# Even output projection and gate projection of a two-layer trunk moved into the convolution's pipeline of seven-product groups

## The chip, the cores and the metric

One core of a Trainium2 chip runs the whole kernel in one launch. The metric is the device time of that launch in microseconds (us). A profiled execution gives, beside its time, a span (first to last instruction), the busy time of each engine, and the chain of work that ended last. Engines: PE (TensorE, matmul), PEld (its weight loads), DVE (VectorE), ACT (ScalarE), POOL (GpSimd), SP (SyncE, which here only issues DMAs). Each engine works through its own instructions strictly in the order in which they stand.

## The reference

Two layers over 2048 tokens of width 1024; all float32. The part that the change touches, cut:

```python
# even layer, end
mix = jnp.concatenate([r * silu(g_ret), y_conv * silu(g_conv)], axis=-1)   # (S, 2048)
y = mix @ w_out                                                              # w_out (2048, 1024)
h = h + rms_norm(y, post_norm[0])
# odd layer, beginning
u = rms_norm(h, pre_norm[1])
cq, ckv, k_rope, gate = split_cols(u @ w_in, (384, 256, 64, 1024))
# ... attention o from cq, ckv, k_rope ...
h = h + rms_norm((o * silu(gate)) @ w_out_odd, post_norm[1])
```

## The kernel before, in words

A float32 product is made of three matmuls: each operand is split into a high part (ACT cast) and a low part (DVE subtraction, `split`), and `mm3` (L86 to L89) adds high·high, high·low and low·high. Stages follow each other: input projection with retention (to about 755 us), convolution (to 1326 us), even output projection (to 1699 us), gate projection (to 1874 us), the other odd projections, attention, the last output projection.

The input projection and the convolution are written as groups of seven products. A group computes a 2x2 block product with seven instead of eight multiplications (Strassen-Winograd): the left operand's four blocks `A11..A22` and sums of them `S1..S4`, the right operand's `B11..B22` and sums `T1..T4`. One product is 12 matmuls of 128x128 by 512 columns (four k tiles, three passes), a group is 84. A step of the pipeline (`step`, one per product, "slot" from here on) first emits the 12 matmuls of its product on PE (`product`), then in `slot`: small PE work (`pe_ev`, such as transposes), the preparation of later products (`prep`: DVE low part for four slots ahead, ACT high part for five, SP load for eight), events of that slot (`at`), copies of partial sums out of PSUM (`keep_x`), and what follows on the small PE work. `conv_engine` then adds the pieces of a finished group on DVE. Sums of the left operands are made ahead by POOL in `job`s: load four blocks, four 128x512 additions (`job_ops`), store to DRAM. `change` loads and splits a new set of seven right operands. As PROD orders the products, P4 and P3 of a group are done inside the next group.

The output projection is written plainly: for each of 16 tiles of 128 tokens, 96 matmuls of 512 columns (`y_mm`, L980; 16 k tiles, three passes, two halves), where the tile's `mix` block is split as it comes and the weights stay split in SBUF. `y_post` makes the two norms of a tile: squares on ACT, `rstd_small` (DVE, then `pow` on POOL), scaling and the residual on DVE, stores `h_d`. `y_tr` transposes the normed tile on PE (8 matmuls, L946), copies it out on ACT and stores it by POOL in `u2t_d`. The gate projection takes four blocks of 512 tokens by 8 column tiles by 24 matmuls; `gate_post` applies Silu on ACT and stores by POOL. Then follows the projection to cq, ckv and k_rope ("d1", L1179 and on: `u_dma`, `u_split`, `wd_dma`, `wd_prep`, `d1_mm`).

Of the kernel before, what the change touches and what calls it, by code (L numbers as in the profile page):

```python
# [64 lines left out]
def body(ctx, tc, x, positions, pre_norm, post_norm, w_heads, w_conv, even_conv_w, even_conv_b, ret_gn,  # L65
# [34 lines left out]
    u2t_d = dram.tile([D, S], F32, name="u2t_d")  # L100
# [20 lines left out]
    identb = const.tile([P, P], BF16, name="identb")  # L121
    amaskb = const.tile([P, P], BF16, name="amaskb")
# [55 lines left out]
    with ExitStack() as es:  # L178
# [6 lines left out]
        j8 = base.tile([P, 2050], F32, name="j8")  # L185
# [7 lines left out]
        NQ_ = RQ + len(CQ)  # L193
# [29 lines left out]
        comb = {i: {} for i in range(6)}  # L223
# [5 lines left out]
        def comb_new(G_, n_):  # L229
# [3 lines left out]
            elif G_ == 4:  # L233
# [4 lines left out]
                comb[G_][n_] = [(*a_, 0, 3), (*views(row3[w_], 1024 * o, 1, 512), 3, 1)]  # L238
            else:
# [12 lines left out]
        def group_of(Q):  # L252
            return Q // 8 if Q < RQ else 4 + (Q - RQ) // 16
# [14 lines left out]

        def item_dma(n_):
# [149 lines left out]
        with ExitStack() as rs_:  # L419
# [453 lines left out]
            def conv_engine(t_):  # L873
# [3 lines left out]
                if j < 5:  # L877
                    if not RQ <= p < NQ_:
                        return
# [31 lines left out]
                elif RQ <= Q < NQ_:  # L911
# [14 lines left out]
        with ExitStack() as cs_:  # L926
            cp = cs_.enter_context(tc.tile_pool(name="cp", bufs=1, reuse_waits="tile"))
            jc = [cp.tile([P, 3072], F32, tag="u8", bufs=1, name="jc0"), cp.tile([P, 2048], F32, name="jc1")]
            for i, (kd, a_, b_) in enumerate([("w", q_, 0) for q_ in range(6, 16)] + [("u", 1, k) for k in range(4)]):
                job_at(LAST_SMALL + 1 + 5 * i, job(kd, a_, b_, jc[i % 2]))  # L930
            change(5, RQ + 16, dict(B11=-14, T1=-6, T2=-4, B21=-2, T3=-1, T4=0, B22=2), dict(B11=-8, T1=-1, T2=1, B21=2, T3=4, T4=5, B22=7))
            for t_ in range(LAST_SMALL + 1, len(SEQ)):
                step(t_)


    mps, mes = ExitStack(), ExitStack()
    psm = mps.enter_context(tc.tile_pool(name="psm", bufs=1, space=PSUM, reuse_waits="tile"))
    mid = mes.enter_context(tc.tile_pool(name="mid", bufs=1, reuse_waits="tile"))

    def y_tr(t, u2):  # L940
        uo = mid.tile([P, KT, P], F32, tag="uo", bufs=1, name=f"uo{t}")
        for j in range(2):
            pt = psm.tile([P, 4, P], F32, tag="tr", bufs=2, name=f"up{t}_{j}")
            for i in range(4):
                k = 4 * j + i
                PE.transpose(pt[:, i, :], u2[:, k * P:(k + 1) * P], ident)  # L946
            A.copy(uo[:, 4 * j:4 * j + 4, :], pt)
        G.dma_start(u2t_d[:, t * P:(t + 1) * P].rearrange("(k p) t -> p k t", p=P), uo)
# [856 lines left out]
```

## Time and profile before

| | |
|---|---|
| time, median of 3 runs (lowest to highest) | 3057.41 us (3056.49 to 3058.24) |
| the profiled execution's own time | 3055.22 us |
| its span | 3053.4 us |
| busy: PE, PEld, DVE, ACT, POOL | 97%, 86%, 59%, 45%, 28% of the span |
| mean granted TensorE clock | 0.992 |

The busy share of PE is a sum over matmuls that overlap each other, so it says that PE is hardly ever without work, not that it is at its peak. To read what a stage costs, look at the distance between the starts of matmuls: a 128x512 matmul is listed with 0.39 us, but the next one starts 0.227 us later. The granted clock is 1.0 at 2.4 GHz and 0.5 at 1.2 GHz.

### The profile page before, as it was taken

How to read it: one execution, taken by the hardware profiler on the slowest of the kernel's cores; microseconds unless marked ns; L12 is line 12 of the kernel's file. 1: busy time of each engine (PE TensorE's matmuls, PEld its weight loads, DVE VectorE, ACT ScalarE, POOL GpSimd, SP SyncE). 2: the span in 40 equal slices, each digit the busy share in tenths (PEclk: the TensorE clock that was granted, in tenths of full speed). 3: DMA queues.
4: the chain of work that ended last, by engine and by line, in shares of the span. 5: the costliest groups of instructions: out<-in, count | busy, mean ns of one | idle time of the engine just before them, and what ended most of it. 6: DMA issues, size and time to landing. Idle time of an engine off the chain costs nothing.

```text
span 3053.4 us, 46275 instructions
## 1 busy us (share of the span) xinstructions
PE 2976.4 (97%) x16425; PEld 2615.8 (86%) x16425; DVE 1788.4 (59%) x3557; ACT 1371.5 (45%) x3312; POOL 849.1 (28%) x1203
## 2 busy tenths in 40 slices
PE   7989999999999999989999999999999999999998
PEld 6878889898888888878888888988899999999887
DVE  7767777767665755553323312577666666666643
ACT  5655555656333533332222322333655555555521
POOL 5554455521442000001111110023333333334210
PEclk9999999999999999999999999999999999999999
DMA  7476777756887633354333624246111212111552
GB/s 294 165 245 209 236 239 246 244 168 220 290 300 226 193 111 111 111 179 143 114 125 108 196 77 135 69 137 227 54 60 53 72 53 67 61 60 56 171 171 85
DMA packets 292246, 463.94 MB, mean 152 GB/s; under 512 B 28432, under 2 KB 183712, under 8 KB 287264
## 3 DMA queue, kind: packets, MB, share of 16 engines
q1 hardware_dynamic: 260208, 376.80, 39.2%
q0 software_dynamic: 22128, 74.99, 6.8%
q10 hardware_dynamic: 9680, 9.20, 0.9%
q8 instruction: 130, 2.13, 0.3%
q14 instruction: 100, 0.82, 0.1%
HBM read 322.49 MB, written 158.07 MB: 157 GB/s over the span
## 4 chain that ended last, share of the span: by engine, by line
PE 89%; DMA 4%; POOL 2%; DVE 2%; ACT 1%; issue 1%; SPq 0%; POOLq 0%; DVEq 0%; ACTq 0%
PE y L980 11%; PE bx L87 6%; PE bx L88 5%; PE bx L89 5%; PE fy L1752 5%; PE T L1557 4%; PE by L87 3%; PE by L88 3%; PE by L89 3%; PE o L1587 2%; PE o L1586 2%; PE o L1585 2%; PE S L1504 2%; PE S L1507 2%; PE S L1508 2%; PE S L1505 2%
## 5 line engine op out<-in xcount | busy, mean ns | idle before, releaser
L1525 POOL TENSOR_SCALAR P<-P,al 128x512 f32<-128x512 f32 (+2 forms) x320 | 220.0, 698 | 352.5 <-DVE al L1530 168.1
L307 DVE TENSOR_TENSOR us<-us 128x512 fp32r<-128x512 f32 x392 | 295.9, 760 | 17.4 <-ACT us L299 14.5
L1515 ACT ACTIVATE P<-S,nm 128x512 f32<-128x512 f32 (+2 forms) x320 | 201.1, 628 | 197.1 <-DVE nm L1512 173.5
L299 ACT CAST us<-us 128x512 fp32r<-128x512 f32 x392 | 235.5, 620 | 103.1 <-DMA us<-s_d 31.8
L1512 DVE TENSOR_REDUCE nm<-S 128x1 f32<-128x512 f32 (+2 forms) x320 | 194.4, 609 | 70.6 <-PE S L1508 42.6
L1561 DVE TENSOR_TENSOR TL<-T,TH 128x512 fp32r<-128x512 f32 x224 | 154.4, 689 | 64.0 <-ACT TH L1560 63.1
L1585 PE MATMUL o<-TH,vH 128*128 128x256 f32 x576 | 185.1, 321 | 0.0
L370 ACT COPY u<-bx 128x512 f32<-128x512 f32 (+1 forms) x124 | 66.1, 533 | 236.7 <-PE bx L89 236.5
L980 PE MATMUL y<-woH,mH 128*128 128x512 f32 x512 | 159.9, 394 | 9.4 <-ACT woH L82 9.4
L1557 PE MATMUL T<-ident,P 128*128 128x128 f32 x1088 | 166.2, 273 | 0.0
L1587 PE MATMUL o<-TH,vL 128*128 128x256 f32 x576 | 162.9, 283 | 0.0
L1586 PE MATMUL o<-TL,vH 128*128 128x256 f32 x576 | 162.1, 281 | 0.0
L980 PE MATMUL y<-woH,mL 128*128 128x512 f32 x512 | 158.2, 391 | 0.0
L980 PE MATMUL y<-woL,mH 128*128 128x512 f32 x512 | 157.6, 389 | 0.0
L83 DVE TENSOR_TENSOR mL<-mr,mH 128x512 fp32r<-128x512 f32 (+1 forms) x72 | 45.3, 630 | 170.2 <-ACT mH L82 170.1
L1560 ACT CAST TH<-T 128x512 fp32r<-128x512 f32 x224 | 131.3, 586 | 24.0 <-PE T L1557 18.9
L1557 PEld LDWEIGHTS T<-ident,P 128*128 128x128 f32 x1088 | 125.1, 140 | 7.8
L910 POOL DMA_DIRECT2D mix_d<-j x32 | 17.8, 556 | 375.6 <-DVE j L909 373.6
L82 ACT CAST mH<-mr 128x512 fp32r<-128x512 f32 (+1 forms) x72 | 40.9, 569 | 176.8 <-issue 93.6
L980 PEld LDWEIGHTS y<-woH,mH 128*128 128x128 f32 x512 | 95.4, 189 | 28.6 <-ACT woH L82 9.8
L1504 PE MATMUL S<-kH,aqn 128*128 128x512 f32 (+2 forms) x320 | 118.4, 370 | 0.1
L1507 PE MATMUL S<-K,aqr 128*128 128x512 f32 (+2 forms) x320 | 115.4, 361 | 0.0
(543 smaller groups left out, 9240.6 us busy)
## 6 DMA issues: line engine op xcount, KB each, us to landing
us<-ws_d SPq DMA_DIRECT2D x128, 256.0 KB, 3.4
us<-s_d SPq DMA_DIRECT2D x96, 256.0 KB, 4.7
us<-wc_d SPq DMA_DIRECT2D x96, 256.0 KB, 2.8
us<-a_d SPq DMA_DIRECT2D x72, 256.0 KB, 4.6
qn_d<-qn POOLq DMA_DIRECT2D x32, 512.0 KB, 3.5
aqn<-qn_d SPq DMA_DIRECT2D x64, 256.0 KB, 3.2
mr<-mix_d SPq DMA_DIRECT2D x56, 256.0 KB, 2.7
jc<-in_even_w_conv SPq DMA_DIRECT2D x40, 256.0 KB, 5.0
```

The lines of the kernel that those rows point to most:

```text
L87: PE.matmul(o, ah, bh, start=first, stop=False, **kw)
L88: PE.matmul(o, ah, bl, start=False, stop=False, **kw)
L89: PE.matmul(o, al, bh, start=False, stop=last, **kw)
L299: A.copy(ring[n_][:, 0], f32(ring[n_][:, 1]))
L307: V.tensor_tensor(out=t_[:, 1], in0=src, in1=f32(t_[:, 0]), op=ALU.subtract)
L980: PE.matmul(ys[t][i], a, w[k][:, i * 512:(i + 1) * 512], start=first and pi == 0, stop=last and pi == 2)
L1515: later(D_EXP, lambda: A.activation(p_[:, 0:w], sp[:, 0:w], AF.Exp, bias=nm[:, j:j + 1], accum_out=sm[:, j:j + 1]))
L1525: G.tensor_scalar(t_[:, 0:ww], t_[:, 0:ww], al[:, jj:jj + 1] if n > 1 else al[:, 5:6], al[:, 5:6] if n > 1 else 1.0, op0=ALU.mult, op1=ALU ...
L1557: PE.transpose(tp[:, e, z, :], src, ident)
L1585: PE.matmul(hold[i], vH[h][:, kb, :], pth[:, c], start=first, stop=False)
L1586: PE.matmul(hold[i], vH[h][:, kb, :], ptl[:, c], start=False, stop=False)
L1587: PE.matmul(hold[i], vL[h][:, kb, :], pth[:, c], start=False, stop=last)
```

## The change

- Output projection: 16 groups of seven products (numbers `CE` to `YE` in the slot count), in two passes of 8. The first pass takes k = 0..1023 (the retention half of `mix`) and stores its result in DRAM (`yp_d`). The second takes k = 1024..2047 and adds the first pass's result, loaded back (`p_in`): three of the four 128x512 additions of a group on POOL (`y_out`), one on DVE.
- Gate projection: 8 groups (from `YE`), with the weights as left operand and the transposed tokens as right operand, each half of the tokens one set of right operands.
- The norms of a finished group of the second pass (two token tiles, tA and tB) run as events of the next group's slots: `y_rstd` (ACT square, then on POOL a multiply-add and a `pow`), `y_h` (DVE scale, POOL residual add of 128x1024, POOL store of `h_d`), `y_rstd` again, `y_u2` (DVE), `y_tr` (8 PE transposes, 8 ACT copies, 2 SP stores to `ub2_d`), and once both tiles are stored `y_sum`: four POOL subtractions in place over the transposed tiles, which give the right operand's sums, and four POOL stores to `tu_d`.
- 20 further jobs in the convolution's slots (sums of `w_out`, of the first half of `mix`, of the gate weights), 8 in the first pass (second half of `mix`), and DRAM copies of `w_out` and of the gate weights into blocks.
- Where an own stage began, with its own tiles and loads, the slots now run on.

Cut diff:

```diff
+        CE = RQ + len(CQ)
+        YE = CE + 16
+        NQ_ = YE + 8
...
+            elif Q >= CE:
+                q_, w = divmod(Q - CE, 8)
+                if i in AIX:
+                    r, kh = divmod(AIX[i], 2)
+                    SP.dma_start(L, mix_rows(q_, kh, 2 * w + r))
+                else:
+                    SP.dma_start(flat(L), ms_d[Q - CE, :, SIX0[i]])
...
+            def y_out(p, r, h, t_, eng):
+                if p < CE + 8:
+                    tok = (2 * (p - CE) + r) * P
+                    eng.dma_start(yp_d[tok:tok + P, h * 512:h * 512 + 512], t_)
+                elif p < YE:
+                    yt = yb["p"][r][:, h * 512:h * 512 + 512]
+                    G.tensor_tensor(out=yt, in0=yt, in1=t_, op=ALU.add)
...
+            def y_rstd(t, i, src):
+                ss = base.tile([P, 1], F32, tag="yss", bufs=3, name=f"yss{t}_{i}")
+                A.activation(yb["u"][t % 2], src, AF.Square, accum_out=ss)
+                G.tensor_scalar(ss, ss, 1.0 / D, EPS, op0=ALU.mult, op1=ALU.add)
+                G.tensor_tensor(out=ss, in0=ss, in1=nhalf[:, 0:1], op=ALU.pow)
...
+            def y_h(t):
+                V.scalar_tensor_tensor(out=yb["u"][r], in0=yb["p"][r], scalar=yrs.pop((t, 0)), in1=yb["g"], ...)
+                G.tensor_tensor(out=yb["x"][r], in0=yb["u"][r], in1=yb["x"][r], op=ALU.add)
+                G.dma_start(h_d[t * P:(t + 1) * P, :], yb["x"][r])
+            def y_u2(t):
+                V.tensor_scalar(yb["u"][t % 2], yb["x"][t % 2], yrs.pop((t, 1)), None, op0=ALU.mult)
+            def y_tr(t):
...
+                            PE.transpose(pts[j][:, i, :], yb["u"][h][:, k * P:(k + 1) * P], ident)
...
+                            A.activation(uo[:, k * P:(k + 1) * P], pts[j][:, i, :], AF.Copy, scale=gcol[:, k:k + 1])
+                        SP.dma_start(ub2_d[half, h, j][:, :, w * P:(w + 1) * P], uo[:, j * 512:(j + 1) * 512]...)
+            def y_sum(w2, i):
+                a_, b_ = yb["o"]
+                b11, b21, b12, b22 = a_[:, 0:512], a_[:, 512:1024], b_[:, 0:512], b_[:, 512:1024]
+                o, x_, y_ = ((b11, b12, b11), (b12, b22, b12), (b22, b22, b11), (b21, b21, b22))[i]
+                G.tensor_tensor(out=o, in0=x_, in1=y_, op=ALU.subtract)
+                if i == 3:
+                    for n_, src in (("T1", b11), ("T3", b12), ("T2", b22), ("T4", b21)):
+                        G.dma_start(tu_d[half, :, TIX[n_], :, w * P:(w + 1) * P], src...)
...
+            for w in range(8):
+                b = T0(CE + 8 + w)
+                n = b + 7
+                at(n - 1, lambda tB=tB: x_in(tB))
+                at(n + 2, lambda tA=tA: x_in(tA))
+                at(n + 2, lambda tB=tB: y_rstd(tB, 0, yb["p"][1]))
+                at(n + 3, lambda tB=tB: y_h(tB))
+                at(n + 5, lambda tB=tB: y_rstd(tB, 1, yb["x"][1]))
+                at(n + 6, lambda tB=tB: y_u2(tB))
+                small(n + 7, *y_tr(tB))
+                at(n + 4, lambda tA=tA: y_rstd(tA, 0, yb["p"][0]))
+                at(n + 5, lambda tA=tA: y_h(tA))
+                at(n + 7, lambda tA=tA: y_rstd(tA, 1, yb["x"][0]))
+                at(n + 8, lambda tA=tA: y_u2(tA))
+                small(n + 9, *y_tr(tA))
+                for i in range(4):
+                    at(n + 10 + i // 2, lambda w=w, i=i: y_sum(w, i))
...
+            for G_, Q in ((6, CE), (7, CE + 8), (8, YE), (9, YE + 4)):
+                change(G_, Q, L6, S6)
...
-        for t in range(NB0, NT):
-            y_alloc(t)
-            nxt = []
-            for k4 in range(4):
-                h, l = cur[k4]
-                for i in range(4):
-                    y_mm(t, h[:, i, :], l[:, i, :], 4 * k4 + i, k4 == 0 and i == 0, k4 == 3 and i == 3)
...
-        for tb in range(4):
-            UH, UL = ubt[tb][:, 0], ubt[tb][:, 1]
-            for c in range(8):
...
-                for k in range(KT):
-                    mm3(pp, H[:, k, :], L[:, k, :], UH[:, k, :], UL[:, k, :], k == 0, k == KT - 1)
```

What the change makes of POOL's order. Before, in the output projection, POOL had these rows for two token tiles (`yrs`: the norms' `pow`; `u2t_d`: store of a transposed tile; `h_d`: store of the residual):

```order
L128 TENSOR_TENSOR yrs_12935<-yrs_12935,nhalf 128x1
L998 DMA h_d<-hh_12930 128x1024
L128 TENSOR_TENSOR yrs_12935<-yrs_12935,nhalf 128x1
L948 DMA u2t_d<-uo_13008 128x8x128
L128 TENSOR_TENSOR yrs_13090<-yrs_13090,nhalf 128x1
L998 DMA h_d<-hh_13085 128x1024
L128 TENSOR_TENSOR yrs_13090<-yrs_13090,nhalf 128x1
L948 DMA u2t_d<-uo_13163 128x8x128
```

The elementwise work of the stage was on DVE. Now, in the second pass, a group's round on POOL begins with these rows (L1085 is `y_sum` of the group before, in place on the transposed tiles `uo`; `yx` is the residual and holds tB in the first row of L1052; `yss` are the norms):

```order
L1085 TENSOR_TENSOR uo<-uo 128x512 x2
L1052 TENSOR_TENSOR yx<-yu,yx 128x1024
L1053 DMA h_d<-yx 128x1024
L998 TENSOR_TENSOR yp<-yp,u_75_14212 128x512
L1085 TENSOR_TENSOR uo<-uo 128x512 x2
L1089 DMA tu_d<-uo 128x4x128 x4
L1045 TENSOR_SCALAR yss_0_14411<-yss_0_14411 128x1
L1046 TENSOR_TENSOR yss_0_14411<-yss_0_14411,nhalf 128x1
L1045 TENSOR_SCALAR yss_1_14435<-yss_1_14435 128x1
L1046 TENSOR_TENSOR yss_1_14435<-yss_1_14435,nhalf 128x1
```

and ends with these (the residual of tA, its second norm, two additions of the next group and the first norm of the next tB), after which the next round's L1085 stands:

```order
L1052 TENSOR_TENSOR yx<-yu,yx 128x1024
L1053 DMA h_d<-yx 128x1024
L1045 TENSOR_SCALAR yss_1_14491<-yss_1_14491 128x1
L1046 TENSOR_TENSOR yss_1_14491<-yss_1_14491,nhalf 128x1
L998 TENSOR_TENSOR yp<-yp,u_76_14462 128x512
L998 TENSOR_TENSOR yp<-yp,p_76_14291 128x512
L1045 TENSOR_SCALAR yss_0_14556<-yss_0_14556 128x1
L1046 TENSOR_TENSOR yss_0_14556<-yss_0_14556,nhalf 128x1
L1085 TENSOR_TENSOR uo<-uo 128x512 x2
```

So the subtractions of one group stand ahead of the norms of the next group on the same engine.

## Rows read from the trace of the kernel before

**Rows 1.** The page: busy time, and PE and its clock in 40 slices.
```profile
PE 2976.4 (97%) x16425; PEld 2615.8 (86%) x16425; DVE 1788.4 (59%) x3557; ACT 1371.5 (45%) x3312; POOL 849.1 (28%) x1203
...
PEclk9999999999999999999999999999999999999999
```
**Rows 2.** Busy time by stretch: length, engines, granted clock, DMA share, GB/s.
```profile
760.00:1000.00 240.00, 240.00 (x1061) 198.79 (x1060) 144.75 (x193) 90.00 (x157) 90.19 (x82) 1.00 0.83 269
1000.00:1326.00 326.00, 325.32 (x1435) 268.81 (x1433) 179.01 (x273) 123.53 (x217) 11.48 (x26) 1.00 0.42 125
1340.00:1700.00 360.00, 360.00 (x1650) 299.19 (x1649) 131.27 (x195) 107.39 (x211) 39.67 (x60) 1.00 0.44 144
1875.00:1895.00 20.00, 17.90 (x102) 15.95 (x101) 6.98 (x11) 8.43 (x21) 1.26 (x2) 1.00 0.63 193
```
**Rows 3.** PE's timeline at two borders of stages: start, length, instruction, idle before.
```profile
1325.94 0.39 PE L89 MATMUL by<-row,us 128*128 128x512 f32 x1
1335.71 2.08 PE L980 MATMUL y<-woH,mH 128*128 128x512 f32 x4 [9.38 <-ACT woH L82]
...
1874.05 0.32 PE L87 MATMUL pa<-wdH,ut 128*128 128x352 f32 x1
```
**Rows 4.** The chain of waits, one token tile: start, length, what.
```profile
1415.41 0.88 PE up L946 x8
1416.28 21.81 PE y L980 x96
```
**Rows 5.** Stretches of 2 us around the wait at 1326 us, as rows 2.
```profile
1326.00:1328.00 2.00, 0.33 (x2) 0.00 (x0) 1.52 (x3) 0.63 (x1) 0.00 (x0) 1.00 0.34 131
1328.00:1330.00 2.00, 0.00 (x0) 0.00 (x0) 0.46 (x1) 0.00 (x0) 0.54 (x1) 0.62 0.07 29
1336.00:1338.00 2.00, 2.00 (x5) 1.55 (x5) 2.00 (x3) 1.10 (x3) 0.00 (x0) 0.50 0.64 246
1338.00:1340.00 2.00, 2.00 (x9) 1.64 (x8) 1.31 (x3) 1.35 (x2) 0.00 (x0) 0.82 0.94 296
```
**Rows 6.** POOL by shape: line, operation, count, busy us, mean ns, idle before.
```profile
L376 POOL TENSOR_TENSOR jc<-jc 128x512 f32<-128x512 f32 x46 | 64.0, 1392 | 19.0 <-DMA jc<-a_d 16.7
L332 POOL TENSOR_TENSOR c2B<-c2B 128x768 fp32r<-128x768 f32 x2 | 4.6, 2290 | 0.0
L948 POOL DMA_DIRECT2D u2t_d<-uo x16 | 14.8, 928 | 76.5 <-ACT uo L947 70.2 <-issue 6.3
L998 POOL DMA_DIRECT2D h_d<-hh x16 | 9.5, 593 | 48.0 <-DVE hh L997 48.0
```
**Rows 7.** POOL's small norm steps: duration ns min/median/max, first and last start.
```profile
L462 POOL TENSOR_SCALAR ss<-ss x16: 189/234/1917, 7.4 to 157.1; 128x1 f32<-128x1 f32 x16
L463 POOL TENSOR_TENSOR ss<-ss,nhalf x16: 550/560/1470, 7.7 to 157.4; 128x1 f32<-128x1 f32 x16
```
**Rows 8.** DVE and ACT by shape, columns as rows 6.
```profile
L1001 DVE SCALAR_TENSOR_TENSOR u<-hh,yrs,gpre 128x1024 f32<-128x1024 f32 x16 | 20.6, 1285 | 11.0 <-POOL yrs L128 11.0
L171 DVE TENSOR_SCALAR nsinT<-sinT 128x512 f32<-128x512 f32 x1 | 0.4, 426 | 0.0
L332 DVE TENSOR_TENSOR c4T<-c4T 128x1024 fp32r<-128x1024 f32 x8 | 9.8, 1222 | 2.8 <-ACT c4T L331 2.6
L914 DVE TENSOR_TENSOR p<-ba,p 128x512 f32<-128x512 f32 x30 | 20.6, 687 | 32.2 <-PE ba L89 32.2
L537 ACT COPY kT<-tr 128x128 f32<-128x128 f32 x64 | 17.1, 267 | 0.7
L331 ACT CAST c4T<-c4T 128x1024 fp32r<-128x1024 f32 x8 | 8.4, 1052 | 0.0
```
**Rows 9.** DMA issues, 1340 to 1720 us: count, KB each, median us to landing.
```profile
mr<-mix_d SPq DMA_DIRECT2D x56, 256.0 KB, 2.7
u2t_d<-uo POOLq DMA_DIRECT2D x16, 512.0 KB, 4.1
u2r<-u2t_d SPq DMA_DIRECT2D x8, 512.0 KB, 6.4
```

More of the change, by code (lines that the diff above doesn't have):

```diff
@@ L99, in body @@
     h_d = dram.tile([S, D], F32, name="h_d")
-    u2t_d = dram.tile([D, S], F32, name="u2t_d")
+    yp_d = dram.tile([S, D], F32, name="yp_d")
+    ub2_d = dram.tile([2, 2, 2, P, 4, 512], F32, name="ub2_d")
+    tu_d = dram.tile([2, P, 4, 4, 512], F32, name="tu_d")
+    ty_d = dram.tile([2, P, 4, 4, 512], F32, name="ty_d")
+    wo_d = dram.tile([2, 2, 2, P, 4, 512], F32, name="wo_d")
+    ms_d = dram.tile([16, P, 4, 512], F32, name="ms_d")
+    gs_d = dram.tile([4, P, 4, 512], F32, name="gs_d")
+    wg_d = dram.tile([8, 2, P, 512], F32, name="wg_d")
     gate_d = dram.tile([D, S], F32, name="gate_d")
@@ L222, in body @@
             crow3[n_] = ((9, o_["B11"])[i // 3], i % 3)
-        comb = {i: {} for i in range(6)}
+        comb = {i: {} for i in range(10)}
         row3 = {}
@@ L877, in conv_engine @@
                 if j < 5:
-                    if not RQ <= p < NQ_:
+                    if not RQ <= p < CE:
                         return
@@ new lines, in y_u2, with pe, en @@
+            def y_u2(t):
+                V.tensor_scalar(yb["u"][t % 2], yb["x"][t % 2], yrs.pop((t, 1)), None, op0=ALU.mult)
+            def y_tr(t):
+                half, w, h = t // 8, (t % 8) // 2, t % 2
+                def pe():
+                    pts = [psb.tile([P, 4, P], F32, tag=tag, bufs=1, name=f"up{t}_{tag}") for tag in ("tr", "sk")]
+                    for j in range(2):
+                        for i in range(4):
+                            k = 4 * j + i
+                            PE.transpose(pts[j][:, i, :], yb["u"][h][:, k * P:(k + 1) * P], ident)
+                    return pts
+                def en(pts):
+                    uo = yb["o"][h]
+                    for j in range(2):
+                        for i in range(4):
+                            k = 4 * j + i
+                            A.activation(uo[:, k * P:(k + 1) * P], pts[j][:, i, :], AF.Copy, scale=gcol[:, k:k + 1])
+                        SP.dma_start(ub2_d[half, h, j][:, :, w * P:(w + 1) * P], uo[:, j * 512:(j + 1) * 512].rearrange("p (k t) -> p k t", k=4))
+                return pe, en
@@ L932, in body @@
+            at(T0(CE) + 6, y_open)
+            at(T0(CE + 8) + 3, y_tiles)
+            at(T0(YE) + 7, g_open)
             for t_ in range(LAST_SMALL + 1, len(SEQ)):
                 step(t_)
-    mps, mes = ExitStack(), ExitStack()
+    mps = ExitStack()
     psm = mps.enter_context(tc.tile_pool(name="psm", bufs=1, space=PSUM, reuse_waits="tile"))
[L938 to L943, printed above, removed]
-            for i in range(4):
[L945 to L948, printed above, removed]
@@ L1133, in body @@
-    mes.close()
     with ExitStack() as oes:
@@ L1168, in body @@
             with ExitStack() as es1:
-                ep = es1.enter_context(tc.tile_pool(name="ep", bufs=1, reuse_waits="tile"))
+                ep = es1.enter_context(tc.tile_pool(name="ep", bufs=1, side="right", reuse_waits="tile"))
                 NQ = QL + KVL + ROPE
@@ L1191, in u_dma @@
                     urr[t] = ep.tile([P, KT, P], F32, tag="ur", bufs=2, name=f"ur{t}")
-                    SP.dma_start(urr[t], u2t_d[:, t * P:(t + 1) * P].rearrange("(k p) t -> p k t", p=P))
+                    for j in range(2):
+                        w = (t % 8) // 2
+                        SP.dma_start(urr[t][:, 4 * j:4 * j + 4, :], ub2_d[t // 8, t % 2, j][:, :, w * P:(w + 1) * P])
                 def u_split(t):
```

297 lines of the change are left out of this document (134 added, 163 removed).

## The prediction, written before the changed kernel ran

> **What bounds the kernel now.** I read the page first: PE is busy 97% of the span, and its clock is full in all 40 slices [rows 1]. So nothing but PE's own work, or a new wait of PE, can move the time much. Then the stretches by stage: PE has no idle time in the convolution nor in the output projection, while POOL works 40 of 360 us in the latter [rows 2]. Then PE's timeline at the borders: the last convolution matmul starts at 1325.94 us, the first of the output projection at 1335.71 after 9.4 us of waiting, the first of d1 at 1874.05 [rows 3]. The chain of waits shows a steady token tile: 96 matmuls in 21.81 us and 8 transposes in 0.88 [rows 4]. That is 0.227 us a matmul, and it is the price of every 512-column matmul below.
>
> **PE's own work.** From the end of the convolution (1325.94 + 0.23) to d1 are 547.9 us. The new stretch has 16 + 8 groups of 84 matmuls, 288 fewer than before, and the same 16 times 8 transposes: 24 x 84 x 0.2272 = 458.0, and 16 x 0.88 = 14.1, together 472.1 us. The gain is 75.8 us, of which 65 are matmuls and the rest the 9.4 us wait with the slow matmuls behind it [rows 3, 5]. This holds only if PE never waits. A group with its 16 transposes takes 19.08 + 1.76 = 20.8 us; this is the pace that the other engines must keep in the second pass.
>
> **First pass and gate groups.** They carry no norms. POOL does at most one job (four additions of 1.39 us [rows 6]) in six slots of 2.7 us, and DVE and ACT have less to do than in the convolution, which ran without a PE wait at a DMA share of 0.83 while the jobs ran [rows 2]. The 20 jobs added there prolong that state, they do not thicken it. I cost all this at nothing; it is hidden behind PE, and if the cover fails, a rival below has the price.
>
> **Second pass: a loop through POOL.** POOL's own work in a round is seven 128x512 operations (9.7 us at 1.39), two of 128x1024, four pairs of small norm steps (0.23 + 0.56 each [rows 7]), two stores of 0.59 and four stores to `tu_d`. For 128x1024 there is no row: not below the 2.29 of 768 columns, and 3.2 if 512 to 768 is extended [rows 6]; I take 2.6, a little under twice the 1.39 of the 512-column row, which is much the larger sample. A `tu_d` store lies between the 0.59 of `h_d` and the 0.93 of `u2t_d`, which has twice its pieces; I take 0.72. The sum is 9.7 + 5.2 + 3.2 + 1.2 + 2.9 = 22.2 us, already over 20.8. But the order makes it worse, since POOL also waits in it: `y_sum` of one group stands ahead of the residual and norms of the next group, and it overwrites `uo`, so it waits until the stores of `uo` to `ub2_d` have landed. Those come last in a chain that began with the very norms that POOL still has to do. Following one round from `y_sum`'s start:
> - POOL: four subtractions, one addition (5 x 1.39 = 6.96), residual of tB 2.6, store 0.59, four `tu_d` stores 2.9, first norm of tA 0.79: 13.8 us.
> - DVE, in order behind that norm: scaling of tA 1.29, a sum out of PSUM 0.69, a low part of about the same form (0.69), then `y_u2` of tB. The last has no row at 1024; twice the 512-column 0.426 is 0.85, the ends are 0.43 and the 1.29 of the scaling [rows 8]. Together 3.5 us. The second norm of tB is done by POOL meanwhile.
> - PE: transposes of tB 0.88, two products 5.45 (they stand between tB and tA), the first four transposes of tA 0.44: 6.8 us.
> - ACT: four copies of 0.267 [rows 8] before the first store: 1.1 us.
> - SP's store of 256 KB in 512-byte pieces: 2.7 as the equally large `mix_d` loads, 4.1 as the twice as large `u2t_d` stores, 6.4 as the `u2r` loads of that stretch [rows 9]. I take 3.4, between the first two, which are nearest in kind.
>
> That is 28.6 us against 20.8. PE stands for the difference in front of tB's transposes: after tA's transposes it has five products (13.6 us) and then nothing, for about 7 to 8 us. Behind it wait all later products, whose inputs are ready. In the 9.4 us wait of before the clock fell to half within 2 to 4 us of the last matmul and was back to full about 3 us after the next [rows 5]; 3.2 us at half rate lose 1.6 us. A wait of 7 us should do the same. The round is then 30.2 us and loses 9.4.
>
> How often: the first group's norms have no `y_sum` ahead of them, so its transposes come in time. From tA of the first to tA of the eighth group are seven rounds: 7 x 9.4 = 66 us. In the last two rounds the split of the gate's first right operands stands among the norms on DVE (1.22 each [rows 8]): one such step in the sixth, and in the seventh a product's operand itself comes late, some 3 us; I add 4.
>
> The Trainium skill ("GPSIMD Engine Reference", section 3.1, Elementwise — side-by-side cycle accounting) speaks against this change: it calls VectorE about twice as fast for elementwise two-input work and gives 4.5 us for an addition of 2048 columns on GpSimd, so, as an estimate from that page, 1.12 for 512 and 2.25 for 1024. The row has 1.39 for 512 [rows 6], beside a busy DVE, so the row decides. By the page's figures a round would be 1.7 us shorter and the time 12 us less, 3043.
>
> **Border to d1.** Before, d1's first operands were ready when the gate ended, and PE lost 20 - 17.9 = 2.1 us later on weights [rows 2]. Now ACT's casts for d1 stand behind the last gate Silu, which waits for PE's last product: DVE sum 0.69, Silu and its store about 1 (an estimate, from the 1.05 of a cast twice as wide), cast of `ut` 1.05 and of `wd` 0.72, then two DVE low parts of 1.22 and 0.84, of which half lies beside ACT (0.72 and 0.84 are scaled from 1024 to 704 columns) [rows 8]. PE loses some 5.5 us, so 3.4 more than before; the bounds are 0 (loads early enough to hide all weights' waits) and 7.
>
> **Sum.** -75.8 + 66 + 4 + 3.4 = -2.4 us. On the profiled execution's 3055.2 that is 3052.8; the median of the runs lies 2.2 above that execution, so 3055.
>
> **Rivals.**
> - *The loop does not bind.* For it: POOL is idle for 320 of 360 us in this stage now, DVE for 229 [rows 2], and PE would only have to wait if POOL is behind. Against it: the order, in which the subtractions precede the next residual, and 22.2 us of POOL work in 20.8. It needs a round under 20.8, so 8 us off the chain; no row is off by so much. Time: 3057.4 - 75.8 + 3.4 = 2985. Between this and my forecast lie rounds of 21 to 27 us.
> - *The loop holds, and its store lands late: slower.* The second pass moves about 7 MB a round (7 operand loads of 256 KB, two loads and a store of 512 KB for each of two tiles, eight stores of 256 KB), over 200 GB/s, more than the 144 of this stretch before [rows 2]. If the store to `ub2_d` takes the 6.4 us of the `u2r` loads, each round is 3 us longer: 21 us more, 3076. It decides from 4.6 us of landing on (1.2 us more in seven rounds bring the time over the bound of "slower").
> - *The convolution starves.* The added jobs and DRAM copies could make left operands late in the second half of the convolution, where DMA had fallen to 0.42. If each of the 20 jobs cost one slot of 2.7 us: 54 us more, 3109. Against it: 760 to 1000 us, the same jobs, PE idle for nothing [rows 2].
> - *The clock holds*, since the waits are shorter than the one of before: 1.6 us a round less, 11 in all, 3044. This is inside my own range.
>
> **How the numbers follow.** The loop binds with its landing near the rows: 0.62, own range 3038 to 3068, from a landing of 2.7 with the clock held (round 27.9, 7 x 7.1 = 50 us) to one of 4.6 with the 1024-column operation at 3.2. The loop does not bind, or hardly: 0.12. Late landing: 0.20. Starved convolution or another new wait: 0.06. A run of this kernel can be told from no change from about 0.2% on, 6.1 us. Faster (below 3051.3): the 0.12 and somewhat over a third of the 0.62, 0.35. Within: 0.26, the largest part of what is left of the 0.62. Slower: 0.39. The range that leaves two in ten outside goes from 3030 to 3085.
>
> **What would show it.** In the profile after: PE gap-free from the convolution into the first pass; then in the second pass PE waits seven times, 6 to 9 us each, released by DVE's `y_u2` (tB), with transposes of tB about 30 us apart and the granted clock at half behind each wait; POOL's longest wait is `y_sum` on the store to `ub2_d`. Gate groups of 19.1 us without waits. I am wrong if the second pass runs at about 21 us a group, if PE waits there for left operands or for PSUM, or if the convolution has waits that it had not.

## The result: slower by 1.5%, and the profile after

| | before | after |
|---|---|---|
| median of the runs on the same chip | 3056.95 us (4 runs) | 3105.2 us (4 runs, 3101.15 to 3105.42) |
| ratio after to before | | 1.0154, interval 1.0137 to 1.0172 |
| profiled execution; span; clock | 3055.22; 3053.4; 0.992 | 3105.31; 3103.2; 0.980 |

The forecast was 3055, range 3030 to 3085: the time lies 50 us above it and outside the range. The page of after, answering [rows 1]: 22.8 us less PE work, 301 us more on POOL, and a dip of the granted clock around slice 20.

```profile
PE 2953.6 (95%) x16137; PEld 2580.9 (83%) x16137; DVE 1972.6 (64%) x3697; ACT 1504.5 (48%) x3596; POOL 1150.3 (37%) x1427
...
PEclk9999999999999999999988899999999999999999
```

By stretch, as [rows 2] (length; PE, PEld, DVE, ACT, POOL; clock, DMA share, GB/s): the convolution (1000 to 1326), the first pass, five rounds of the second pass, its end, the gate groups.

```profile
1000.00:1326.00 326.00, 318.25 (x1384) 260.58 (x1383) 207.28 (x268) 124.78 (x216) 106.67 (x90) 0.99 0.80 255
1340.00:1480.00 140.00, 137.50 (x599) 111.75 (x598) 77.56 (x90) 54.29 (x94) 54.62 (x53) 1.00 0.98 303
...
1560.00:1680.00 120.00, 94.31 (x385) 75.50 (x384) 56.36 (x60) 53.10 (x132) 83.39 (x86) 0.87 0.72 219
1680.00:1790.00 110.00, 78.53 (x316) 61.02 (x315) 56.45 (x64) 57.87 (x127) 69.96 (x67) 0.84 0.76 253
1790.00:1890.00 100.00, 97.33 (x420) 78.18 (x419) 50.69 (x71) 54.70 (x92) 5.93 (x6) 1.00 0.76 234
```

PE waits for a fifth to over a quarter of the second pass, and the granted clock is 0.84 to 0.87 there. The convolution, which had no wait, has 7.7 us of them, at nearly twice the DMA share it had (0.80 against 0.42 in [rows 2]). The three largest waits of PE in the second pass (engine, line, waited for: us, times, longest). The first is product P7 waiting for ACT's copy of a partial sum, the second tB's transposes, the third product P2 (bank `ba`) waiting for a right operand's high part:

```profile
PE bx L87 <- ACT u L403: 37.7, 7, 8.6
PE up_tr L1066 <- DVE yu L1056: 10.8, 5, 2.9
PE ba L87 <- ACT c4T L364: 10.6, 1, 10.6
```

and the two largest of POOL in the same stretch:

```profile
POOL uo L1085 <- DMA ub_d<-uo: 54.5, 8, 11.1
POOL yss L1045 <- ACT yu L1044: 18.1, 13, 3.1
```

The 54.5 us are `y_sum` waiting for the stores of `uo` to land: the loop that was forecast. One round of it, from POOL's timeline (start, length, instruction, idle before and its releaser). It begins and ends with `y_sum`:

```profile
1646.46 3.09 POOL L1085 TENSOR_TENSOR uo<-uo 128x512 f32<-128x512 f32 x2 [4.83 <-DMA ub_d<-uo]
1649.51 2.36 POOL L1052 TENSOR_TENSOR yx<-yu,yx 128x1024 f32<-128x1024 f32 x1
...
1660.41 0.56 POOL L1046 TENSOR_TENSOR yss<-yss,nhalf 128x1 f32<-128x1 f32 x1
1661.05 1.28 POOL L1045 TENSOR_SCALAR yss<-yss 128x1 f32<-128x1 f32 x1
1662.42 0.55 POOL L1046 TENSOR_TENSOR yss<-yss,nhalf 128x1 f32<-128x1 f32 x1
1662.93 2.76 POOL L1052 TENSOR_TENSOR yx<-yu,yx 128x1024 f32<-128x1024 f32 x1
...
1679.48 1.66 POOL L1085 TENSOR_TENSOR uo<-uo 128x512 f32<-128x512 f32 x1 [4.88 <-DMA ub_d<-uo]
```

The same round on DVE,

```profile
1661.00 1.29 DVE L1051 SCALAR_TENSOR_TENSOR yu<-yp,yss 128x1024 f32<-128x1024 f32 x1 [13.97 <-POOL yss L1046]
1662.20 0.68 DVE L1036 TENSOR_TENSOR p<-ba,p 128x512 f32<-128x512 f32 x1
1662.81 0.68 DVE L336 TENSOR_TENSOR us<-us 128x512 fp32r<-128x512 f32 x1
1663.40 2.84 DVE L1056 TENSOR_SCALAR yu<-yx,yss 128x1024 f32<-128x1024 f32 x1
```

on ACT (the square at 1654.14 ends ACT's wait for POOL; the copy at 1655.19 behind it is the one that PE waits for),

```profile
1654.14 1.06 ACT L1044 ACTIVATE yu<-yp 128x1024 f32<-128x1024 f32 x1 [8.93 <-POOL yp L998]
1655.10 0.18 ACT L1044 ACTIVATION_READ_ACCUMULATOR yu<-yp 128x1 f32 x1
1655.19 0.57 ACT L403 COPY u<-bx 128x512 f32<-128x512 f32 x1
...
1674.98 1.14 ACT L1074 ACTIVATE uo<-up_tr,gcol 128x128 f32<-128x128 f32 x4 [1.28 <-issue]
```

on PE, at its two waits and at tA's transposes,

```profile
1655.81 0.79 PE L87 MATMUL bx<-c4B,us 128*128 128x512 f32 x1 [5.27 <-ACT u L403]
...
1666.30 0.66 PE L1066 MATMUL up_tr<-ident,yu 128*128 128x128 f32 x4 [2.54 <-DVE yu L1056]
...
1674.29 0.60 PE L1066 MATMUL up_tr<-ident,yu 128*128 128x128 f32 x4
```

and the store on SP:

```profile
1676.14 2.07 SPq L1075 DMA_DIRECT2D ub_d<-uo  x2
```

The clock behind PE's first wait, as stretches of 2 us:

```profile
1656.00:1658.00 2.00, 2.00 (x5) 1.61 (x6) 0.00 (x0) 1.83 (x4) 1.60 (x3) 0.50 0.01 2
...
1662.00:1664.00 2.00, 1.75 (x8) 1.09 (x6) 2.00 (x4) 0.11 (x1) 1.92 (x3) 1.00 0.38 109
```

Read it as a chain in which each engine waits for the one before: POOL 14.5 us (1646.46 to 1660.97), DVE 5.3 (to 1666.24), PE 8.7 (to ACT's copies at 1674.98, with the first product at the half clock), ACT 1.2, store 3.3 (1676.14 to 1679.48): 33.0 us, against 30.2 forecast and 20.8 wanted.

**The ledger**, from starts of matmuls on PE's timeline. The seven rounds, transposes of tA to transposes of tA, take 31.2, 33.5, 32.2, 33.0, 31.0, 38.8 and 36.2: 235.9 us, 90.0 more than 7 x 20.84. Where right operands change, groups stand further apart than 19.1: 11.2 us lost in the convolution (30.5 from group to group; 19.3 before), 4.0 at the first pass, 4.2 at the second, 4.7 inside the gate. The norms of the second pass's first group, ahead of the seven rounds, lose 2.5, most of it PE waiting at P7. d1's first matmul waits 4.3. Together 120.9 us of losses, less the 75.8 of PE work: 45.1 of the 49.1 us by which d1 starts later (1923.16, against the 1874.05 of [rows 3]); the rest is spread.

### The profile page after: what moved, and what is told of

Its sections match the earlier page's. It is cut to its first block, busy times and chain, and to the rows that moved or that the text cites. A ratio compares the mean times of both kernels' runs of the same rounds, so it can differ in the third digit from the quotient of the medians.

```text
span 3103.2 us, 47313 instructions
## 1 busy us (share of the span) xinstructions
PE 2953.6 (95%) x16137; PEld 2580.9 (83%) x16137; DVE 1972.6 (64%) x3697; ACT 1504.5 (48%) x3596; POOL 1150.3 (37%) x1427
## 4 chain that ended last, share of the span: by engine, by line
PE 76%; DMA 7%; POOL 6%; issue 5%; DVE 4%; ACT 2%; SPq 1%; POOLq 0%; ACTq 0%; DVEq 0%
PE bx L87 7%; PE bx L88 7%; PE bx L89 7%; PE fy L1783 5%; PE by L87 4%; PE T L1588 4%; PE by L88 4%; PE by L89 4%; PE o L1617 2%; PE o L1618 2%; PE o L1616 2%; PE S L1535 2%; PE S L1538 2%; PE S L1539 2%; PE S L1536 2%
## 5 line engine op out<-in xcount | busy, mean ns | idle before, releaser
L336 DVE TENSOR_TENSOR us<-us 128x512 fp32r<-128x512 f32 x560 | 460.8, 831 | 70.1 <-ACT us L328 66.8
L328 ACT CAST us<-us 128x512 fp32r<-128x512 f32 x560 | 339.5, 623 | 203.9 <-DMA us<-wc_d 38.1
L1546 ACT ACTIVATE P<-S,nm 128x512 f32<-128x512 f32 (+2 forms) x320 | 200.7, 627 | 196.7 <-DVE nm L1543 173.1
L403 ACT COPY u<-bx 128x512 f32<-128x512 f32 (+1 forms) x172 | 94.0, 546 | 293.8 <-PE bx L89 293.5
L409 POOL TENSOR_TENSOR jc<-jc 128x512 f32<-128x512 f32 x138 | 198.5, 1438 | 42.2 <-DMA jc<-in_even_w_out 14.6
L87 PE MATMUL bx<-c4T,us 128*128 128x512 f32 x384 | 152.8, 398 | 1.7 <-ACT c4T L364 1.0
L88 PE MATMUL bx<-c4T,us 128*128 128x512 f32 x384 | 151.5, 394 | 1.0 <-DVE c4T L365 0.8
L89 PE MATMUL bx<-c4T,us 128*128 128x512 f32 x384 | 151.1, 393 | 0.0
L1535 PE MATMUL S<-kH,aqn 128*128 128x512 f32 (+2 forms) x320 | 118.4, 370 | 0.1
L1538 PE MATMUL S<-K,aqr 128*128 128x512 f32 (+2 forms) x320 | 115.5, 361 | 0.0
L1536 PE MATMUL S<-kL,aqn 128*128 128x512 f32 (+2 forms) x320 | 115.3, 360 | 0.0
L1539 PE MATMUL S<-K,aqr 128*128 128x512 f32 (+2 forms) x320 | 115.2, 360 | 0.0
L1537 PE MATMUL S<-kH,aqn 128*128 128x512 f32 (+2 forms) x320 | 115.0, 359 | 0.0
```

Source lines behind the costliest of these rows:

```text
L87: PE.matmul(o, ah, bh, start=first, stop=False, **kw)
L88: PE.matmul(o, ah, bl, start=False, stop=False, **kw)
L89: PE.matmul(o, al, bh, start=False, stop=last, **kw)
L328: A.copy(ring[n_][:, 0], f32(ring[n_][:, 1]))
L336: V.tensor_tensor(out=t_[:, 1], in0=src, in1=f32(t_[:, 0]), op=ALU.subtract)
L1546: later(D_EXP, lambda: A.activation(p_[:, 0:w], sp[:, 0:w], AF.Exp, bias=nm[:, j:j + 1], accum_out=sm[:, j:j + 1]))
```

## The experiments

Measured times are medians beside runs of the kernel before on the same chip; the seven rounds are read as above, from the one profiled execution of each run. Names of waits: P7 is the product of the first wait in the list above. A theory or rival keeps its letter through all expectations.

| run | time, us | ratio to before, interval | seven rounds, us |
|---|---|---|---|
| changed kernel | 3105.2 | 1.0154, 1.0137 to 1.0172 | 235.9 |
| e1_nosub | 3037.3 | 0.9934, 0.9916 to 0.9951 | 168.0 |
| e2_sep | 3099.7 | 1.0141, 1.0126 to 1.0156 | 213.1 |
| e3_late | 3089.1 | 1.0108, 1.0093 to 1.0123 | 200.7 |
| e4_rstd | 3115.9 | 1.0197, 1.0181 to 1.0212 | 248.4 |
| e5_stt | 3106.8 | 1.0161, 1.0146 to 1.0176 | 239.7 |
| e6_jobs | 3101.4 | 1.0144, 1.0126 to 1.0162 | 236.1 |
| e7_dve | 3066.7 | 1.0034, 1.0022 to 1.0045 | 183.0 |
| e9_best | 3067.5 | 1.0036, 1.0025 to 1.0046 | 185.5 |
| e10_gap40 | 3100.0 | 1.0142, 1.0128 to 1.0155 | 233.3 |
| e11_ring9 | 3039.6 | 0.9947, 0.9932 to 0.9962 | 172.2 |
| e12_best | 3035.2 | 0.9929, 0.9916 to 0.9941 | 172.2 |

### The loop

**e1_nosub.**
```diff
-                G.tensor_tensor(out=o, in0=x_, in1=y_, op=ALU.subtract)
```


> Left out: the four POOL subtractions of y_sum in each of the eight groups of the second pass; the four stores to tu_d stay and carry unsummed blocks, so the gate's sums are wrong. All transfers stay. Theory L (the loop: y_sum waits on POOL for the stores of uo to have landed, and the next group's norms wait behind it): without the write in place the stores to tu_d need only ACT's copies, the chain per round falls from about 33 to under 20, and the rounds of the second pass go back to about 21 to 22 us instead of 31 to 39: 75 to 90 us less, 3015 to 3030. Rival A (ACT's order: the copy of a finished product's partial sum stands behind the square of tA, which waits for POOL's addition): most of the 5 to 6 us wait in front of product P7 stays in each round, about 35 to 45 us of the 90: 3060 to 3070. Rival D (full DMA queues): the traffic is the same, so the rounds stay at 31 to 39 us: 3100 to 3110.

Five rounds of 22.0 to 22.2 us, then 28.1 and 29.5; 67.9 us less in the rounds and as much in the time, which at 3037.3 lies above the 3015 to 3030 of theory L. Five rounds are where L put them, and rivals A and D fall: the wait at P7 is gone and the traffic is all there. But the edit also takes the subtractions' own work from POOL (4 x 1.34 us a round), so it does not tell the wait from that work; e2 and e3 do. The last two rounds were to be 21 to 22 and are not. The DMA share is near 1 in the five rounds already and 1.03 with the gate's right operands on top (stretches as above); in the last two rounds PE waits for the high and low parts of those operands:

```profile
1628.00:1650.00 22.00, 21.10 (x101) 17.31 (x102) 15.06 (x16) 13.96 (x35) 17.83 (x20) 1.00 0.96 321
...
1670.00:1680.00 10.00, 6.74 (x22) 4.99 (x21) 6.46 (x7) 6.39 (x14) 3.52 (x4) 0.66 1.03 401
```

**e2_sep.**
```diff
-                o, x_, y_ = ((b11, b12, b11), (b12, b22, b12), (b22, b22, b11), (b21, b21, b22))[i]
+                o, x_, y_ = ((s1, b12, b11), (s3, b22, b12), (s2, b22, s1), (s4, b21, s2))[i]
...
-            return base.tile([P, 2, 4, P], F32R, tag="us", bufs=9, name=f"us{n_}")
+            return base.tile([P, 2, 4, P], F32R, tag="us", bufs=8, name=f"us{n_}")
```


> y_sum writes to a tile of its own, so it no longer waits for the stores of uo to land, only for ACT's copies; order on POOL and all work unchanged (one load buffer of nine is given up for the space). Theory L: the landing leaves the loop, 3.2 us in the clean rounds less up to 1.1 for the second half of the copies, 7 to 8 in the last two less the same: 2 to 3.2 us in five rounds and 5.5 to 6.5 in two, together 21 to 29: 3076 to 3084. If POOL's load alone (22.7 us a round) set the pace, the rounds would be near 23 already, and this edit would change nothing: 3105. Rival A: the square waits for POOL's addition, which moves forward with y_sum by the same amount, so it gives the same as L here. Rival D: nothing, 3100 to 3110.

The rounds are 22.8 us shorter, inside the 21 to 29 of L: the landing was in the loop, and POOL's load alone did not set the pace. The time missed (5.5 us less instead of 21 to 29), since the space was not free: the transposes of the first tA come 14 us later than in the changed kernel, lost ahead of the second pass, some 9 of them at the changes of right operands. That eight load buffers reach less far than nine is argued here (see e11).

**e3_late** (on top of e2's edit).
```diff
-                    at(n + 10 + i // 2, lambda w=w, i=i: y_sum(w, i))
+                    at(n + 13, lambda w=w, i=i: y_sum(w, i))
+                at(n + 16, lambda w=w: y_tu(w))
```


> The separate tile, and y_sum's four subtractions three slots later on POOL (behind the next group's first norms and residuals), its stores to tu_d three slots behind that; POOL's work is the same to the instruction. Theory L: the loop is open, what is left is POOL's own work of 22.7 us a round: seven rounds at 22.7 to 24 instead of 33.7 on average, 68 to 77 us less: 3028 to 3037. POOL's load alone as the cause of after's rounds: nothing changes, 3105. Rival D: nothing, 3100 to 3110. Rival A: the POOL additions come earlier, so the square does; up to 40 us less, 3065.

The steady rounds fall to 27.4 us, not to 22.7 to 24: 35 us less in the seven instead of 68 to 77, and with the 14 us of the missing load buffer on top the time is 3089.1, far from 3028 to 3037. The loop is open (no wait of POOL on a store is left), yet POOL, in order, still waits for short detours through ACT's squares and DVE's scaling, as its waits over six rounds show:

```profile
POOL yss L1046 <- ACT yu L1045: 14.9, 12, 1.3
POOL yx L1053 <- DVE yu L1052: 8.4, 6, 1.4
```

Those and the 0.3 before each `h_d` store make some 4.5 us a round, which leaves 22.9 of the 27.4 for POOL's own work. So the steady rounds had two parts: about 5 us a round that the order of `y_sum` cost, and a POOL that could not have kept 20.8 anyway. The work itself is stretched: the subtractions now run beside DVE's low parts of left operands (L336, 0.68 us when alone), and the two hold each other up. One such low part, and POOL's four subtractions around it:

```profile
1601.45 4.82 DVE L336 TENSOR_TENSOR us<-us 128x512 fp32r<-128x512 f32 x1
1601.93 2.54 POOL L1087 TENSOR_TENSOR ysm<-uo 128x512 f32<-128x512 f32 x2
1604.43 3.01 POOL L1087 TENSOR_TENSOR ysm<-uo,ysm 128x512 f32<-128x512 f32 x2
```

**e4_rstd.**
```diff
-                at(n + 4, lambda tA=tA: y_rstd(tA, 0, yb["p"][0]))
+                at(n + 5, lambda tA=tA: y_rstd(tA, 0, yb["p"][0]))
```


> Only the first norm of tA (its square on ACT, its two small steps on POOL) stands one slot later, so that the copy that product P7 waits for no longer stands behind the square on ACT. Theory L: PE's wait goes from P7 to the transposes of tB, which stand on the loop; the round stays at 33.7 on average within 1 us: 3098 to 3112. Rival A: the 5 to 6.2 us wait at P7 goes in seven rounds and does not come back: 35 to 43 us less, 3062 to 3070.

```profile
PE up_tr L1066 <- DVE yu L1056: 51.6, 5, 10.7
```

The 37.7 us on ACT's copy are gone. In the first five rounds all of PE's wait stands at tB's transposes, 10.3 on average, and these rounds are 0.3 to 3 us longer. The time is 10.7 longer, 3115.9, and the rounds are 35.5 on average instead of 33.7: more than the 3098 to 3112 and the 1 us that theory L allowed. Rival A falls: ACT's order decided where PE waits, the loop decided how long.

**e5_stt.**
```diff
-                V.tensor_scalar(yb["u"][t % 2], yb["x"][t % 2], yrs.pop((t, 1)), None, op0=ALU.mult)
+                V.scalar_tensor_tensor(out=yb["u"][t % 2], in0=yb["x"][t % 2], scalar=yrs.pop((t, 1)), in1=yb["g"], ...)
```


> y_u2 as a SCALAR_TENSOR_TENSOR that multiplies by post_norm as well (a factor too many: the transposed tokens differ from the reference's). The changed kernel has 2.84 us for the TENSOR_SCALAR of tB in the loop, beside a running POOL addition, and 0.74 for its shortest one; the SCALAR_TENSOR_TENSOR of y_h has 1.29 beside the same POOL. Theory P (that form waits until POOL's running instruction ends): the new form takes 1.3, each round of the loop is 1.5 us shorter, 10 us in all: 3093 to 3097. Rival (any DVE instruction that starts while POOL works on 1024 columns is held up): it takes 2.5 to 2.9 again, 3103 to 3107.

Theory P falls, the rival holds: no time is won. Durations (min, median, max in ns) of `y_u2` in the changed kernel,

```profile
L1056 DVE TENSOR_SCALAR yu<-yx,yss x16: 741/1778/2892, 1535.0 to 1777.8; 128x1024 f32<-128x1024 f32 x16
```

and here:

```profile
L1056 DVE SCALAR_TENSOR_TENSOR yu<-yx,yss,yp x16: 1272/2312/3424, 1530.3 to 1777.5; 128x1024 f32<-128x1024 f32 x16
```

Both forms have their longest 2.15 us above their shortest. The shortest are the ones beside which POOL runs no addition; the longest (2.83 to 2.89 us and 3.36 to 3.42) all start beside POOL's 128x1024 addition and end 0.55 or 1.1 us behind it. So both forms are held up by that addition.

### The changes of right operands

**e6_jobs**, and **e10_gap40** with 40 for 25.
```diff
-                job_at(LAST_SMALL + 1 + 5 * i, job(kd, a_, b_, jc[i % 2]))
+                job_at(LAST_SMALL + 1 + 5 * i + (25 if i >= 14 else 0), job(kd, a_, b_, jc[i % 2]))
```


> The twenty added jobs of the convolution start 25 slots later, so that none runs while the right operands of the convolution's second half are loaded and split. Theory Q (jobs and operand loads together fill the DMA queues, share 0.99 to 1.05 there): the 11.2 us that the changed kernel loses at that place go, 3092 to 3096; if the late jobs press on the first pass, some 2 to 4 us come back there. Rival (the split order on ACT and DVE alone loses them): no change, 3103 to 3107.

> The gap in the convolution's jobs again, 40 slots instead of 25: with 25 the first late jobs (loads of w_out, 3.9 us to land) still ran at 1010 to 1050 us, beside the operand loads, with a DMA share of 0.97 to 1.01, and the change of operands cost 28.4 us there instead of 30.5. Theory Q: with no job in that stretch the share falls to that of the kernel before, the two groups' distance falls from 30.5 to 19.1 to 20.5, 10 to 11 us less: 3092 to 3097. Rival (the order of splits on ACT and DVE alone): distance 28 to 31 again, 3100 to 3106.

With 25 the distance at the change was 28.4 us and the time 3.8 us lower, a miss: the first late jobs still fell into the stretch. With 40 it is 19.4, as theory Q said, while the time, 3100.0, lies in the rival's 3100 to 3106. The stretch 1020 to 1050 in the changed kernel,

```profile
1020.00:1050.00 30.00, 22.25 (x83) 16.51 (x82) 21.07 (x29) 15.41 (x25) 6.81 (x7) 0.89 0.99 316
```

and with the gap of 40:

```profile
1020.00:1050.00 30.00, 30.00 (x132) 24.47 (x131) 27.47 (x41) 19.33 (x32) 1.49 (x3) 1.00 0.68 220
```

In the changed kernel ACT waited there for left operands to land (1010 to 1062 us; a further 6.7 us for `ws_d`), and none of these waits is left with the gap of 40:

```profile
ACT us L328 <- DMA us<-wc_d: 9.3, 4, 6.5
```

So the jobs beside the operand loads cost the 11.2 us, by their traffic, and theory Q holds in its place. In the time only 5 of them show: the jobs now end at the first pass, where the next change of operands takes 10 us in place of 4. More than half is given back there.

### Versions meant to be faster

**e7_dve** and **e9_best** (the part of the edit that both share, again on top of e2's tile).
```diff
-                G.tensor_tensor(out=o, in0=x_, in1=y_, op=ALU.subtract)
+                V.tensor_tensor(out=o, in0=x_, in1=y_, op=ALU.subtract)
...
-                    at(n + 10 + i // 2, lambda w=w, i=i: y_sum(w, i))
+                    at(n + 12, lambda w=w, i=i: y_sum(w, i))
+                at(n + 14, lambda w=w: y_tu(w))
```


> y_sum's subtractions on DVE into a tile of their own, two slots later, its stores to tu_d two slots behind; POOL keeps 17.3 us a round. By theory L and the run without subtractions (five rounds of 22.0, two of 28 and 29.6 with full DMA queues) the seven rounds take about 169 us instead of 235.9, 67 less; the room for the tile (one load buffer of nine given up) costs the 14 us that the two runs with such a tile lost ahead of the second pass: 3045 to 3058. If DVE, with 2.8 us a round more, or its stalls beside POOL set the pace: rounds of 24 to 26, 3065 to 3080.

> The version with the subtractions on DVE, with the gap of 25 slots in the convolution's jobs, and y_u2 as a TENSOR_TENSOR with the norm broadcast over the columns. Adding the parts: 67 us less in the second pass, 11 less in the convolution, 0 to 5 less from y_u2 (the loop that it stood on is open, so mostly hidden), 14 more for the load buffer: 3036 to 3046, faster than both kernels. If the DMA queues are the limit the gap only moves traffic into the first pass: 3045 to 3055.

The first takes 3066.7, above its 3045 to 3058 and inside the 3065 to 3080 given for DVE or its stalls as the pace: one round of 21.1, four of 23.4 to 24.5, and 30 and 37 at the end. Which of the two holds it back was not told apart: DVE's low parts of left operands take 1.18 us on average (0.73 in the changed kernel), and ACT now waits for left operands, whose median landing has gone from 5.2 us in the changed kernel (count, KB each, landing),

```profile
us<-ms_d SPq DMA_DIRECT2D x16, 256.0 KB, 5.2
```

to 7.2:

```profile
us<-ms_d SPq DMA_DIRECT2D x17, 256.0 KB, 7.2
```

The second gains nothing on it (3067.5, expected 3036 to 3046): its first five rounds are about 0.5 us longer, and so is the broadcast `y_u2` (median 2.86 us for ten, against 2.33), and the gap of 25 slots was too short, as above.

**e11_ring9** and **e12_best** (the second with the gap of 40).
```diff
-                V.scalar_tensor_tensor(out=yb["u"][r], in0=yb["p"][r], scalar=yrs.pop((t, 0)), in1=yb["g"], ...)
-                G.tensor_tensor(out=yb["x"][r], in0=yb["u"][r], in1=yb["x"][r], op=ALU.add)
+                V.scalar_tensor_tensor(out=yb["p"][r], in0=yb["p"][r], scalar=yrs.pop((t, 0)), in1=yb["g"], ...)
+                G.tensor_tensor(out=yb["x"][r], in0=yb["p"][r], in1=yb["x"][r], op=ALU.add)
...
-                o, x_, y_ = ((b11, b12, b11), (b12, b22, b12), (b22, b22, b11), (b21, b21, b22))[i]
-                G.tensor_tensor(out=o, in0=x_, in1=y_, op=ALU.subtract)
+                o, x_, y_ = ((s1, b12, b11), (b12, b22, b12), (b22, b22, s1), (s4, b21, b22))[i]
+                V.tensor_tensor(out=o, in0=x_, in1=y_, op=ALU.subtract)
...
-                        G.dma_start(tu_d[half, :, TIX[n_], :, w * P:(w + 1) * P], src...)
+                        SP.dma_start(tu_d[half, :, TIX[n_], :, w * P:(w + 1) * P], src...)
```


> Subtractions on DVE two slots later as in the version on DVE, but without giving up a load buffer: two sums go over tB's transposed tile (its stores landed long before), two into room won by scaling the norm's input in place and writing the squares nobody reads elsewhere; the four stores to tu_d on SP instead of POOL. If the 14 us that the versions with a tile of their own lost ahead of the second pass come from the missing buffer: the starts up to the second pass are those of the changed kernel within 3 us, rounds 22 to 23.5, 3048 to 3058. If they come from something else: 3060 to 3068.

> The same with the gap of 40 slots in the convolution's jobs. By both theories 10 to 11 us less than the version without the gap: 3038 to 3048, below the kernel before. If the convolution's loss does not come from the jobs: 3048 to 3058, no difference from the kernel before that can be told.

Both beat the expectation, and both kernels: 3039.6 and 3035.2, the latter 0.71% under before (interval 0.59 to 0.84%). In e11 the first tA's transposes are back at 1542.35 us (1544.38 in the changed kernel), so the 14 us came with the tile of its own and the load buffer given up for it; the edit takes back both at once. POOL's four stores moved to SP and tB's load of the first pass's result stands a slot later in the same edit, so what that gave to the rounds was not told apart. In e12 the steady rounds are 21.5 to 22.2 and the last two 26.4 and 36.1, in a second pass at a DMA share of 1.02:

```profile
1560.00:1670.00 110.00, 102.94 (x481) 84.17 (x480) 94.78 (x97) 70.47 (x170) 80.12 (x73) 0.98 1.02 332
```

Full queues do not show as what sets these 22 us. In the five steady rounds PE's only wait is still the one for tB's `y_u2`, 0.8 us a round of the 1.1 above 20.84. ACT waits for left operands twice, 1.5 us in all:

```profile
PE up_tr L1069 <- DVE yu L1059: 4.1, 5, 1.1
ACT us L328 <- DMA us<-ms_d: 1.5, 2, 1.2
```

POOL waits 1.3 us a round there for the load of the first pass's result, which may be the queues' share of it; no run took traffic away. In the last two rounds PE waits for the low and high parts of the gate's right operands, and loads of these land in 7 to 10 us.

## Why the prediction was wrong

- **PE's own work, 75.8 us less:** held. Gate and first-pass groups run at 19.12 us where no operands change.
- **The mechanism, a loop through POOL:** held, link by link in the round shown and by e2 and e3. What lay under it was not seen: with the loop open POOL needs 27.4 us a round, own work and short waits together (e3), where the prediction had 22.2. The loop's size was the first mis-sized term: 66 + 4 forecast, 90.0 measured. In the round shown, POOL took 14.5 instead of 13.8, DVE 5.3 instead of 3.5, PE to the copies 8.7 instead of 8.4 with the half clock, ACT 1.2 for 1.1, the store 3.3 for 3.4: 2.8 us more a round. Some 2 us of that are `y_u2`, taken at 0.85 as twice a row in which POOL did nothing; beside POOL's residual addition it takes 2.84. Neither end of its bounds (0.43 and 1.29) held it: beside none of the rows used was a POOL addition at work.
- **The last two rounds:** 4 us were added for the splits of the gate's operands; they cost 10.6 more than two clean rounds of 32.2. There the store landed in 7.0 and 7.8 us instead of 2.6 to 4.5, so the rival of the late landing came true in two rounds of seven. The operand that the prediction saw coming 3 us late made PE wait 10.6 us, but through the loop: its cast stood on ACT behind tA's square, which waited for POOL.

```profile
1761.33 1.06 ACT L1044 ACTIVATE yu<-yp 128x1024 f32<-128x1024 f32 x1 [11.09 <-POOL yp L998]
1762.38 0.60 ACT L364 CAST c4T<-c4T 128x512 fp32r<-128x512 f32 x1
```

- **"I cost all this at nothing"** (the convolution, first pass and gate groups) is the step that failed. It took the share of 0.83 of another stretch [rows 2] as proof and did not ask what the added jobs meet in the half of the convolution to which they move: a change of right operands, beside which the share was already at 1.02 before. It cost 11.2 us there (e10), and the changes at the later borders some 13; what part of these 13 is traffic was not tested. The rival on the convolution (0.06) had the right resource and the wrong place: the groups behind the change run at 19.12. A row of before that was not read (1020 to 1030 us) shows the full queues, though they cost before only 0.2 us:

```profile
1020.00:1030.00 10.00, 10.00 (x46) 8.29 (x45) 9.04 (x14) 6.23 (x11) 0.54 (x1) 1.00 1.02 339
```

- **Border to d1:** 4.3 and 0.8 us of wait, 5.5 forecast. Held, with luck: the terms listed (0.69, 1, 1.05, 0.72 and half of 1.22 + 0.84) add up to 4.5, not 5.5.
- **What would show it:** POOL's longest wait, and the half clock behind PE's waits, came as said (0.50 from 1656 to 1658 us, behind the wait of 5.27). PE's waits were two a round, mostly in front of P7, not one at tB; e4 shows that ACT's order sets the place and that moving it wins no time. One of the signs of being wrong came, too: 7.7 us of waits in the convolution.
- The estimate of the Trainium skill ("GPSIMD Engine Reference", section 3.1) of 1.12 and 2.25 us for additions of 512 and 1024 columns fell short of what ran here, 1.34 and 2.51 on average (last figure before the bar's idle time, in ns), and so did the 3043 that it would have given:

```profile
L1085 POOL TENSOR_TENSOR uo<-uo 128x512 f32<-128x512 f32 x30 | 40.2, 1338 | 55.6 <-DMA ub_d<-uo 54.5
L1052 POOL TENSOR_TENSOR yx<-yu,yx 128x1024 f32<-128x1024 f32 x14 | 35.2, 2512 | 0.0
```

The sum: of the 50 us that were missed, 20 are the loop's, 24 those of the operand changes costed at nothing and 2.5 those of the second pass's first norms; the rest is spread.

## What to carry to other kernels

When work is put into a running pipeline, follow each new in-order engine once round its own loop: a write in place that waits for a store makes everything queued behind it wait. Then ask what the engine needs with the loop open. Then look at where the added transfers land in time, against the bursts that are already there (operand changes), not against a stage's mean share. Price an elementwise step from a row with the same neighbour at work.

## What the hardware showed that I had not expected

Some DVE instructions and a POOL addition hold each other up for nearly their whole length: `y_u2` began at 1663.40 while POOL's addition ran from 1662.93 to 1665.69, and ended 0.55 us after it, where it takes 0.74 in all without a POOL addition beside it. It works the other way too: POOL's 128x1 step at 1661.05 took 1.28 us instead of 0.19 while DVE's 1.29 us scaling ran from 1661.00. Nor did DVE get in between POOL's instructions where these followed each other closely: the low part shown under e3 (4.82 us for 0.68) ended 0.56 us after the third subtraction. A DVE sum of a PSUM and an SBUF operand (L1013 at 1606.19 in e3), beside the fourth, took its usual 0.68. The Trainium skill says so ("SBUF — State Buffer", section "Who interferes with whom"): a DVE instruction with two SBUF inputs contends with a GpSimd instruction that reads SBUF, one in a two-port mode contends with GpSimd too, and whichever issues first has the shared ports for its whole instruction while the other is blocked. These rows and e5 agree; worked into the forecast, it would have let `y_u2` take up to POOL's whole addition longer.
